# Samples' recurrent states in three pairs of buffers, with each pair's update one step behind its product with C

## Chip, core and metric

The kernel runs on one core of one Trainium2 chip. The metric is device time in microseconds (us) of one execution, taken as the median of several runs. Engines are named as in the profile: PE (TensorE; PEld is its weight load), DVE (VectorE), ACT (ScalarE), POOL (GpSimd) and SP (SyncE, which here only issues DMAs).

## Reference, cut to what matters

One decoder layer is applied to 256 prompt tokens and to 8 samples of 8 new tokens each, 320 token columns in all. The layer is `x + RMSNorm(W_out [chunkMLP | SSD])`, followed by `x + RMSNorm(ConvFFN)`. The change lies in the SSD part (a state-space recurrence) of the eight samples. There are 32 heads in 4 groups of 8; a head has a state of 64 x 128 numbers per sample, and a group has one B and one C vector (128 numbers) per token:

```
h_t = exp(dt_t a) h_{t-1} + dt_t x_t B_t^T        y_t = h_t C_t
```

Written for all 8 tokens of a sample at once, the kernel needs two things of each old state h: the product of h with the sample's C (a part of y), and the new state `h * exp(sum of dt a) + sum over tokens of (decay dt x) B^T`, which is an output (`ssm_state_sample`).

## The kernel before

**Tiling.** All activations lie transposed: 128 features on the partitions, 320 tokens along the row. Every weight is fetched in slabs of 128 x 1024 fp32 (`slab`, L108 to L119). SP issues the load into `wraw`; ACT casts it to a rounded part `whi` (L117); DVE subtracts to get the rest `wlo` (L119); PE makes three matmuls per 128 x 128 block (`accumulate`, L128 to L130). Each of these three tiles has three buffers, and each slab feeds 24 matmuls. These slabs have a raised priority in the scheduler.

**Order of the work.** `project` (PSUM tiles `ps`) multiplies the input by 512 columns of a weight, and `chunk_out` (PSUM tiles `pd`) multiplies 512 mixed features by W_out. Both call `tick()` between slabs. A tick advances the first generator in the list `bg` to its next `yield`, so the small work of the SSD is strewn between the large matmuls. From 440 us of the span on, the program is: `heads_in(1)` (the convolution's projection of the next group, 5 ticks), `chunk_out` 3 (16 ticks), `heads_out(0)` (the projection z, 12 ticks), and so on around for groups 1 to 3. Each group's `ssd(g)` is one generator; `z_evac` drains what is left of it (`finish(tasks[g])`). The scheduler that lays the instructions out (one fixed order per engine) goes by priority and by when operands and buffers come free, so a load whose buffer is free may be issued well ahead of its place in the program.

**The states.** A state tile `st` is 128 x 512 fp32 (256 KB): one sample, one group. Samples i and 4+i form pair i. Five buffers hold `st`. `ssd(g)` does:

- `load_state(i)` (L729): SP loads the two tiles of a pair.
- `fourfold` (L353): ACT copies the sample columns of x (for one group) and of B (once, at the start) four times over, for the 32 tokens of one half of the samples; PE then transposes (`by_token`, L351). One tile `x4` of 4 KB per partition holds both halves.
- `times` (L746): DVE multiplies a transposed x in PSUM by dt; `xq` is the result for the samples and shares the buffer of `x4`. ACT casts all of `xq` to `xsp` (L788), and DVE subtracts on 64 partitions (L789). `xsp` is the moving operand of every state update of the group.
- `decayed` (L780): POOL makes `xde`, one buffer, which PE multiplies for the prompt's state (`s1`, L797).
- For each pair i: `picked` (L811, ACT: B masked to the sample), `with_c` (L803, PE: C times the pair, into `ps_yo`), `shrunk` (L816, POOL: the state times its decay), `grown` (L821, PE makes `up_ps`, DVE adds it to the state), `store_state` (L828, ACT issues the two stores), then the load of pair i+2. Two yields per pair.
- `ps_yo` goes into `xdt` (L861); then eight heads of decay matrices (`decays`, L870, with their rows `cs` loaded by SP in `load_sums`) and `products` (L890, `y_ps`, L898).

**The last group.** For g = 3 the loop does only `with_c`. The generator `renewals` loads all of group 3's states a second time and updates them during `chunk_out` 6 and 7; its last pair is updated in the hand-over between the two halves of the layer, where `next(rest[0])` (L1004) stands and POOL issues the stores.

Of the kernel before, what the change touches and what calls it, by code (L numbers as in the profile page):

```python
# [2 lines left out]

# [6 lines left out]
F32 = mybir.dt.float32  # L10
F32R = mybir.dt.float32r
I32 = mybir.dt.int32
AF = mybir.ActivationFunctionType
ALU = mybir.AluOpType
# [3 lines left out]
P = 128  # L18
NP = 256
NB, TS = 8, 8  # L20
NS = NB * TS
NT = NP + NS
# [12 lines left out]
def hybrid_step(  # L35
# [10 lines left out]
    act, dve, pool, pe, sp = nc.scalar, nc.vector, nc.gpsimd, nc.tensor, nc.sync  # L46
# [10 lines left out]
    def misc(name):  # L57
        return ms.tile([P, 512], F32, tag="ms", name=name)
# [79 lines left out]
    bg = []  # L138
# [210 lines left out]
    def by_token(ps, x, c):  # L349

        pe.transpose(ps, x[:, P * c:P * c + P], ident)  # L351

    def fourfold(out, x):  # L353

        for i in range(2):
            act.copy(out[:, :, i], x[:, :, 32 * i:32 * i + 32].unsqueeze(2).to_broadcast([P, 4, 4, 32]))
        return out.rearrange("p k i q t -> p k (i q t)")

    with ExitStack() as mctx:
        op = mctx.enter_context(tc.tile_pool(name="op", bufs=1))  # L360
# [335 lines left out]
        with tc.tile_pool(name="sd", bufs=1) as sd:  # L696
# [4 lines left out]
            cb, cms = shared[:, :NT + NS], shared[:, NT + NS:].rearrange("p (b i) -> p b i", b=NB)  # L701
            pool.tensor_copy(cb[:NS, :NS], ident[:NS, :NS])
            pool.tensor_copy(cb[NS:, NT:], ident[NS:, NS:])
            x4 = fourfold(sd.tile([P, 4, 2, 4, 32], F32, tag="x4", name="b4", bufs=1), bT[:, :, NP:NT])
            for c in range(4):
                ps = misc("bt_ps")
                for g in range(4):
                    by_token(ps[:, P * g:P * g + P], (bT if c < 2 else x4)[:, g], c % 2)
                if c < 2:
                    act.copy(btok[:, c, :], ps)  # L710
                else:
                    b = bsp[:, c - 2]
                    act.copy(b, ps)
                    for rs in (slice(32, 64), slice(96, P)):
                        dve.tensor_tensor(out=b[rs], in0=ps[rs], in1=b[rs].bitcast(F32), op=ALU.subtract)

            def by_head(ap):
                return ap.rearrange("p (h d) -> p h d", d=64)
# [4 lines left out]
            def ssd(g):  # L723
# [4 lines left out]

                def load_state(i):  # L729

                    st = [sd.tile([P, 512], F32, tag="st", name="st", bufs=5) for _ in range(2)]
                    for h in range(2):
                        sp.dma_start(st[h], state_ssm[4 * h + i, g])
                    return st
# [5 lines left out]
                    sp.dma_start(cs, dacs_d[h0 + 2 * j:h0 + 2 * j + 2, o:o + NT].unsqueeze(0).broadcast_to([P, 2, NT]))  # L740
                    return cs

                sts = [load_state(i) for i in range(2)]

                xdt = sd.tile([P, 3, 512], F32, tag="xdt", name="xdt", bufs=1)
                def times(out, ps, c, at=slice(0, P), h=slice(0, 8)):  # L746
                    n = h.stop - h.start
                    dve.tensor_tensor(out=by_head(out), in0=by_head(ps),
                                      in1=dt[at, c, h0 + h.start:h0 + h.stop].unsqueeze(2).to_broadcast([at.stop - at.start, n, 64]), op=ALU.mult)
                x4 = fourfold(sd.tile([P, 4, 2, 4, 32], F32, tag="x4", name="x4", bufs=1), xs[:, :, NP:NT])  # L750
                turned = []
                for c in range(4):
                    ps = misc("xt_ps")
                    for j in range(4):
                        by_token(ps[:, P * j:P * j + P], (xs if c < 2 else x4)[:, j], c % 2)
                    if c < 2:
                        times(xdt[:, c, :], ps, c)
                    else:
                        turned.append(ps)
                xq = sd.tile([P, 2, 512], F32, tag="x4", name="xq", bufs=1)  # L760
                for i, ps in enumerate(turned):
                    times(xq[:, i, :], ps, 3 + i)
                    for r in range(2):
                        at = slice(64 - 64 * r + 32 * i, 96 - 64 * r + 32 * i)
                        times(xdt[at, 2, 256 * r:256 * r + 256], ps[at, 256 * r:256 * r + 256], 2, at, slice(4 * r, 4 * r + 4))
# [12 lines left out]
                yield  # L778

                def decayed(i, c):  # L780
                    xde = sd.tile([P, 512], F32, tag="xde", name="xde", bufs=1)
                    pool.tensor_tensor(out=by_head(xde), in0=by_head(xdt[:, c, :]),
                                      in1=dec[:, i, h0:h0 + 8].unsqueeze(2).to_broadcast([P, 8, 64]), op=ALU.mult)
                    return xde

                x0d = decayed(0, 0)
                xsp = sd.tile([P, 2, 512], F32R, tag="xsp", name="xsp", bufs=1)
                act.copy(xsp, xq)  # L788
                dve.tensor_tensor(out=xsp[64:], in0=xq[64:], in1=xsp[64:].bitcast(F32), op=ALU.subtract)  # L789
                for hb in range(2):  # L790
                    dve.tensor_tensor(out=cms[:, 4 * hb:4 * hb + 4], in0=cmask[:, 4 * hb:4 * hb + 4],
                                      in1=cT[:, g, NP + 32 * hb:NP + 32 * hb + 32].unsqueeze(1).to_broadcast([P, 4, 32]),
# [18 lines left out]
                def picked(i):  # L811
                    bm = sd.tile([P, 2, P], F32R, tag="bm", name="bm", bufs=2)
                    act.activation(bm, bsp[:, :, bs].bitcast(F32), AF.Copy, scale=bsel[:, i:i + 1])
                    return bm

                def shrunk(i, st):  # L816
                    for h in range(2):
                        pool.tensor_tensor(out=by_head(st[h]), in0=by_head(st[h]),
                                           in1=tote[:, h0:h0 + 8, 4 * h + i:4 * h + i + 1].to_broadcast([P, 8, 64]), op=ALU.mult)

                def grown(st, bm):  # L821
                    for h in range(2):
                        ps = misc("up_ps")
                        made = pe.matmul(ps, bm[:, h], xsp[:, h], start=True, stop=True)
                        dve.tensor_tensor(out=st[h], in0=st[h], in1=ps, op=ALU.add)
                    return made.ins

                def store_state(i, st, by=act):  # L828
                    for h in range(2):
                        by.dma_start(o_ssm_s[4 * h + i, g], st[h])  # L830

                def renewals():
                    sts = [load_state(i) for i in range(2)]
                    yield
                    for i in range(4):
                        st, bm = sts.pop(0), picked(i)
                        shrunk(i, st)
                        yield
                        made = grown(st, bm)
                        store_state(i, st, act if i < 3 else pool)  # L840
                        if i < 2:
                            sts.append(load_state(2 + i))
                        yield made

                for i in range(4):
                    if g < 3:
                        bm = picked(i)
                    yield
                    st = sts.pop(0)
                    with_c(i, st)  # L850
                    yield
                    if g < 3:
                        shrunk(i, st)
                        grown(st, bm)
                        store_state(i, st)
                    if i < 2:
                        sts.append(load_state(2 + i))

                for r in range(2):
                    at = slice(64 * r, 64 * r + 64)  # L860
                    dve.tensor_tensor(out=by_head(xdt[at, 2, 256 * r:256 * r + 256]), in0=by_head(ps_yo[at, :256]),  # L861
                                      in1=ed[at, g, :].unsqueeze(2).to_broadcast([64, 4, 64]), op=ALU.mult)

                made = {}

# [61 lines left out]
                    (pool if g == 3 else act).dma_start(o_ssm_p[g], s1)  # L927
                    yield
                if g == 3:
                    rest.extend([renewals(), final()])  # L930
                    next(rest[0])
                else:
                    yield
                    yield
                    for _ in final():
                        pass
# [49 lines left out]
            norm = heads_out(2, 2, 3)  # L986
            norm3 = heads_out(3, 3, 2)
            finish(norm)
            bg.append(chain(repeat(None, 1), islice(rest[0], 4)))
            chunk_out(w_out, 6, *res[2], False, rate=2)  # L990
            finish(norm3)
            sq2 = hp.tile([P, NT], F32, tag="ssq", name="sq2")

            bg.append(islice(rest[0], 3))
            squares, one = squares_of(sq2)
            chunk_out(w_out, 7, *res[3], False, squares)

# [3 lines left out]

            with first():
                with tc.issue_after(pd_last[-1]):
                    made = next(rest[0])  # L1004
                with tc.issue_after(made):
                    most = token_sums(sq2)
                with tc.issue_after(sums_ins[-1]):
                    ps = token_sums(*one)
                with tc.issue_after(sums_ins[-1]):
                    made = next(rest[1])  # L1010
                r = rsqrt_by_root(most, ps, 1.0 / D)
                behind = rsqrt_ins[-1]
                with tc.issue_after(behind):
                    next(rest[1])
                with tc.issue_after(made):
                    r2b = spread(r)
# [254 lines left out]
```

## Time and profile before

| what | value |
|---|---|
| median of 3 runs | 1811.76 us (1810.66 to 1812.52) |
| profiled execution, device time | 1810.5 us |
| its span, first to last instruction | 1808.8 us |
| PE, PEld busy | 1781.4 us (98%), 1743.8 us (96%) |
| DVE, ACT, POOL busy | 1183.7, 793.7, 294.7 us |
| granted PE clock, mean | 0.995 |
| DMA | 294.66 MB, mean 163 GB/s |
| loads of `st` | 40 of 256 KB, median 3.9 us from issue to landing |
| stores of `st` | 32 of 256 KB |

How to read it: the times of the profile belong to one execution, whose own time is 1.7 us above its span and 1.3 us below the median. A busy time can hide waits of other engines; where a wait matters is seen in the stretch of time where it falls. The SSD work of the four groups lies between 440 and 750 us of the span, the updates of group 3 between 808 and 853 us.

### The profile page before, as it was taken

The numbers are of one execution on the slowest core, as the hardware profiler recorded it, in microseconds if no ns is written. First come the engines' busy times: TensorE is split into PE (matmuls) and PEld (weight loads), VectorE is DVE, ScalarE is ACT, GpSimd is POOL, SyncE is SP. The second block draws the span as 40 slices with busy tenths as digits, with TensorE's granted clock in tenths as the row PEclk, the third lists the DMA queues.
The fourth block names the chain that finished last, engine by engine and source line by source line (L and its number), as shares of the span: only waits on it lengthen the run. The fifth ranks groups of instructions, "written<-read, shape, count | busy, mean of one in ns | idle before, by whom it ended". The sixth has DMA issues, their size and how long they took to land.

```text
span 1808.8 us, 31156 instructions
## 1 busy us (share of the span) xinstructions
PE 1781.4 (98%) x12200; PEld 1743.8 (96%) x12200; DVE 1183.7 (65%) x2044; ACT 793.7 (44%) x1100; POOL 294.7 (16%) x619
## 2 busy tenths in 40 slices
PE   8999999999999999999999999999999999999998
PEld 7999999999889889999999999999999999999997
DVE  4449664556977968677885464747565565756575
ACT  5444454334535445444554433333434343433335
POOL 2102200000431312104421010101101010101004
PEclk9999999999999999999999999999999999999999
DMA  8656544555565565546554545455545445554542
GB/s 270 187 142 188 171 133 153 153 155 176 196 192 187 165 203 172 159 156 212 161 155 154 154 147 153 148 153 153 154 152 153 145 154 150 155 150 152 149 151 103
DMA packets 222947, 294.66 MB, mean 163 GB/s; under 512 B 16752, under 2 KB 150736, under 8 KB 222608
## 3 DMA queue, kind: packets, MB, share of 16 engines
q1 hardware_dynamic: 210544, 270.21, 49.6%
q10 hardware_dynamic: 9872, 14.82, 2.2%
q0 software_dynamic: 2384, 7.64, 1.4%
q8 instruction: 96, 1.57, 0.4%
q14 instruction: 51, 0.42, 0.1%
HBM read 277.80 MB, written 14.82 MB: 162 GB/s over the span
## 4 chain that ended last, share of the span: by engine, by line
PE 89%; DVE 5%; DMA 3%; issue 1%; ACT 1%; POOL 1%; SPq 0%; ACTq 0%; DVEq 0%; POOLq 0%
PE ps L128 19%; PE ps L130 19%; PE ps L129 19%; PE pd L128 9%; PE pd L130 9%; PE pd L129 9%; DVE wlo L119 2%; DMA cT<-in_x_tok 1%; DMA st<-in_state_ssm 1%; PE y_ps L898 1%; DMA cs<-dacs_d 1%; DMA out_ssm_state_sample<-st 0%; DVE cv L383 0%; DVE cs L883 0%; PE sg L660 0%
## 5 line engine op out<-in xcount | busy, mean ns | idle before, releaser
L119 DVE TENSOR_TENSOR wlo<-wraw,whi 128x1024 fp32r<-128x1024 f32 (+1 forms) x474 | 589.5, 1244 | 443.1 <-ACT whi L117 440.4
L117 ACT CAST whi<-wraw 128x1024 fp32r<-128x1024 f32 (+1 forms) x474 | 494.3, 1043 | 724.7 <-PE ps L129 427.9
L128 PE MATMUL ps<-h_hi,whi 128*128 128x320 f32 x2528 | 786.1, 311 | 5.5 <-ACT whi L117 2.4
L130 PE MATMUL ps<-h_hi,wlo 128*128 128x320 f32 x2528 | 782.8, 310 | 2.5 <-DVE wlo L119 2.5
L129 PE MATMUL ps<-h_lo,whi 128*128 128x320 f32 x2528 | 781.9, 309 | 0.0
L128 PEld LDWEIGHTS ps<-h_hi,whi 128*128 128x128 f32 x2528 | 476.3, 189 | 11.2 <-issue 4.3
L130 PEld LDWEIGHTS ps<-h_hi,wlo 128*128 128x128 f32 x2528 | 476.2, 188 | 4.4 <-DVE wlo L119 4.3
L129 PEld LDWEIGHTS ps<-h_lo,whi 128*128 128x128 f32 x2528 | 476.4, 188 | 0.8 <-issue 0.5
L128 PE MATMUL pd<-fhi,whi 128*128 128x320 f32 x704 | 217.0, 308 | 0.0
L129 PE MATMUL pd<-flo,whi 128*128 128x320 f32 x704 | 217.0, 308 | 0.0
L130 PE MATMUL pd<-fhi,wlo 128*128 128x320 f32 x704 | 217.0, 308 | 0.0
L128 PE MATMUL pd<-ohi,whi 128*128 128x320 f32 x448 | 140.2, 313 | 0.0
L129 PE MATMUL pd<-olo,whi 128*128 128x320 f32 x448 | 138.9, 310 | 0.0
L130 PE MATMUL pd<-ohi,wlo 128*128 128x320 f32 x448 | 138.7, 310 | 0.0
L128 PEld LDWEIGHTS pd<-fhi,whi 128*128 128x128 f32 x704 | 132.1, 188 | 0.0
L129 PEld LDWEIGHTS pd<-flo,whi 128*128 128x128 f32 x704 | 132.1, 188 | 0.0
L130 PEld LDWEIGHTS pd<-fhi,wlo 128*128 128x128 f32 x704 | 132.1, 188 | 0.0
L1082 POOL COPY ptf<-pad 128x2 f32<-128x2 f32 x88 | 21.1, 240 | 620.6 <-DVE pad L1070 620.0
L211 DVE TENSOR_TENSOR acc_ffn<-acc_ffn,pd 128x320 f32<-128x320 f32 x160 | 77.4, 484 | 38.3 <-PE pd L130 36.8
L128 PEld LDWEIGHTS pd<-ohi,whi 128*128 128x128 f32 x448 | 84.1, 188 | 2.9 <-issue 1.6
L130 PEld LDWEIGHTS pd<-ohi,wlo 128*128 128x128 f32 x448 | 84.1, 188 | 1.0 <-issue 1.0
L129 PEld LDWEIGHTS pd<-olo,whi 128*128 128x128 f32 x448 | 84.2, 188 | 0.5 <-issue 0.2
(295 smaller groups left out, 1578.7 us busy)
## 6 DMA issues: line engine op xcount, KB each, us to landing
wraw<-in_ffn_w_up SPq DMA_DIRECT2D x176, 512.0 KB, 3.7
wraw<-in_w_in SPq DMA_DIRECT2D x144, 512.0 KB, 3.8
wraw<-in_ffn_w_down SPq DMA_DIRECT2D x88, 512.0 KB, 3.5
wraw<-in_w_out SPq DMA_DIRECT2D x64, 512.0 KB, 3.5
st<-in_state_ssm SPq DMA_DIRECT2D x40, 256.0 KB, 3.9
out_ssm_state_sample<-st ACTq DMA_DIRECT2D x30, 256.0 KB, 4.0
cs<-dacs_d SPq DMA_DIRECT2D x16, 320.0 KB, 4.5
xr<-in_xT SPq DMA_DIRECT2D x4, 640.0 KB, 4.8
```

Source lines behind the costliest of these rows:

```text
L117: act.copy(hi[:, :m], raw[:, :m])
L119: dve.tensor_tensor(out=lo[:, :m], in0=raw[:, :m], in1=hi[:, :m].bitcast(F32), op=ALU.subtract)
L128: pe.matmul(ps, whi, xhi, start=first, stop=False)
L129: pe.matmul(ps, whi, xlo, start=False, stop=False)
L130: return pe.matmul(ps, wlo, xhi, start=False, stop=last).ins
L211: dve.tensor_tensor(out=acc[:, nb, :], in0=acc[:, nb, :], in1=ps[:, :NT], op=ALU.add)
L898: pe.matmul(ps[64 * i:64 * i + 64, cols], w(hl), x(hl, m, cpx), tile_position=(0, 64 * i), **flags)
L1082: pool.tensor_copy(ptf[:, k, :], pad[:, 256:258])
```

## The change

There are six buffers for `st` (three whole pairs) in place of five, and three pairs are loaded at a group's start. A step of the loop now does `begin(i)` (C times pair i, the mask of B, the decay of the state on POOL) and then `end(i-1)` (update and store of the pair before). The fourth pair is loaded in step 3, when nothing else is begun; it is begun after the loop and ended one tick later. Group 3 does the same as the others, except that its last `end` stays in the hand-over; the second load of its states (`renewals`) and the places that advanced it are gone. A group has two more yields (24 in place of 22 for g < 3, 21 in place of 20 for g = 3).

The room comes from `x4`: `fourfold` now copies one half (i = 0 or 1) into a 2 KB tile with the tag `xde`, which has two buffers instead of one and also holds `xq` (one half) and the products of `decayed`. The cast to `xsp` and the subtraction are made per half, right after that half's `times`, ahead of the group's first yield.

```diff
-    def fourfold(out, x):
-        for i in range(2):
-            act.copy(out[:, :, i], x[:, :, 32 * i:32 * i + 32].unsqueeze(2).to_broadcast([P, 4, 4, 32]))
-        return out.rearrange("p k i q t -> p k (i q t)")
+    def fourfold(out, x, i):
+        act.copy(out.rearrange("p k (q t) -> p k q t", q=4), x[:, :, NP + 32 * i:NP + 32 * i + 32].unsqueeze(2).to_broadcast([P, 4, 4, 32]))
+        return out
...
-            x4 = fourfold(sd.tile([P, 4, 2, 4, 32], F32, tag="x4", name="b4", bufs=1), bT[:, :, NP:NT])
             for c in range(4):
                 ps = misc("bt_ps")
+                b4 = bT if c < 2 else fourfold(sd.tile([P, 4, P], F32, tag="xde", name="b4", bufs=2), bT, c - 2)
                 for g in range(4):
-                    by_token(ps[:, P * g:P * g + P], (bT if c < 2 else x4)[:, g], c % 2)
+                    by_token(ps[:, P * g:P * g + P], b4[:, g], c if c < 2 else 0)
...
-                    st = [sd.tile([P, 512], F32, tag="st", name="st", bufs=5) for _ in range(2)]
+                    st = [sd.tile([P, 512], F32, tag="st", name="st", bufs=6) for _ in range(2)]
...
-                sts = [load_state(i) for i in range(2)]
+                sts = [load_state(i) for i in range(3)]
...
-                x4 = fourfold(sd.tile([P, 4, 2, 4, 32], F32, tag="x4", name="x4", bufs=1), xs[:, :, NP:NT])
-                turned = []
+                xsp = sd.tile([P, 2, 512], F32R, tag="xsp", name="xsp", bufs=1)
                 for c in range(4):
                     ps = misc("xt_ps")
+                    x4 = xs if c < 2 else fourfold(sd.tile([P, 4, P], F32, tag="xde", name="x4", bufs=2), xs, c - 2)
                     for j in range(4):
-                        by_token(ps[:, P * j:P * j + P], (xs if c < 2 else x4)[:, j], c % 2)
+                        by_token(ps[:, P * j:P * j + P], x4[:, j], c if c < 2 else 0)
                     if c < 2:
                         times(xdt[:, c, :], ps, c)
-                    else:
-                        turned.append(ps)
-                xq = sd.tile([P, 2, 512], F32, tag="x4", name="xq", bufs=1)
-                for i, ps in enumerate(turned):
-                    times(xq[:, i, :], ps, 3 + i)
+                        continue
+                    i = c - 2
+                    xq = sd.tile([P, 512], F32, tag="xde", name="xq", bufs=2)
+                    times(xq, ps, c + 1)
+                    act.copy(xsp[:, i], xq)
+                    dve.tensor_tensor(out=xsp[64:, i], in0=xq[64:], in1=xsp[64:, i].bitcast(F32), op=ALU.subtract)
...
-                    xde = sd.tile([P, 512], F32, tag="xde", name="xde", bufs=1)
+                    xde = sd.tile([P, 512], F32, tag="xde", name="xde", bufs=2)
...
-                xsp = sd.tile([P, 2, 512], F32R, tag="xsp", name="xsp", bufs=1)
-                act.copy(xsp, xq)
-                dve.tensor_tensor(out=xsp[64:], in0=xq[64:], in1=xsp[64:].bitcast(F32), op=ALU.subtract)
...
-                def renewals():
-                    sts = [load_state(i) for i in range(2)]
-                    yield
-                    for i in range(4):
-                        st, bm = sts.pop(0), picked(i)
-                        shrunk(i, st)
-                        yield
-                        made = grown(st, bm)
-                        store_state(i, st, act if i < 3 else pool)
-                        if i < 2:
-                            sts.append(load_state(2 + i))
-                        yield made
-
-                for i in range(4):
-                    if g < 3:
-                        bm = picked(i)
-                    yield
-                    st = sts.pop(0)
-                    with_c(i, st)
-                    yield
-                    if g < 3:
-                        shrunk(i, st)
-                        grown(st, bm)
-                        store_state(i, st)
-                    if i < 2:
-                        sts.append(load_state(2 + i))
-
-                for r in range(2):
...
+                def yo_to_xdt():
+                    for r in range(2):
...
+                bms = {}
+
+                def begin(i):
+                    with_c(i, sts[i])
+                    bms[i] = picked(i)
+                    shrunk(i, sts[i])
+
+                def end(i, by=act):
+                    made = grown(sts[i], bms.pop(i))
+                    store_state(i, sts[i], by)
+                    return made
+
+                for i in range(4):
+                    if i < 3:
+                        begin(i)
+                    else:
+                        sts.append(load_state(3))
+                    if i:
+                        end(i - 1)
+                    yield
+                    yield
+                begin(3)
+                yo_to_xdt()
+                yield
+                if g < 3:
+                    end(3)
+                    yield
...
-                    rest.extend([renewals(), final()])
-                    next(rest[0])
+                    rest.extend([lambda: end(3, pool), final()])
...
-            bg.append(chain(repeat(None, 1), islice(rest[0], 4)))
             chunk_out(w_out, 6, *res[2], False, rate=2)
...
-            bg.append(islice(rest[0], 3))
...
-                    made = next(rest[0])
+                    made = rest[0]()
```

More of the change, by code (lines that the diff above doesn't have):

```diff
@@ L1 @@
 from contextlib import ExitStack, nullcontext
-from itertools import chain, islice, repeat
+from itertools import repeat
 import concourse.bass as bass
@@ L845, in ssd @@
-                for i in range(4):
-                    if g < 3:
-                        bm = picked(i)
-                    yield
-                    st = sts.pop(0)
-                    with_c(i, st)
-                    yield
-                    if g < 3:
-                        shrunk(i, st)
-                        grown(st, bm)
-                        store_state(i, st)
-                    if i < 2:
-                        sts.append(load_state(2 + i))
-                for r in range(2):
-                    at = slice(64 * r, 64 * r + 64)
-                    dve.tensor_tensor(out=by_head(xdt[at, 2, 256 * r:256 * r + 256]), in0=by_head(ps_yo[at, :256]),
-                                      in1=ed[at, g, :].unsqueeze(2).to_broadcast([64, 4, 64]), op=ALU.mult)
+                def yo_to_xdt():
+                    for r in range(2):
+                        at = slice(64 * r, 64 * r + 64)
+                        dve.tensor_tensor(out=by_head(xdt[at, 2, 256 * r:256 * r + 256]), in0=by_head(ps_yo[at, :256]),
+                                          in1=ed[at, g, :].unsqueeze(2).to_broadcast([64, 4, 64]), op=ALU.mult)
```

## Prediction

> **What bounds the kernel now.** I read the page first. Section 1 gives the busy time of each engine:
>
> ```profile
> span 1808.8 us, 31156 instructions
> PE 1781.4 (98%) x12200; PEld 1743.8 (96%) x12200; DVE 1183.7 (65%) x2044; ACT 793.7 (44%) x1100; POOL 294.7 (16%) x619
> ```
>
> PE is the bound, and PE's own work stays: the change has the same transposes, products with C and updates. So a gain can only come out of the 27 us in which PE is idle. The second view, busy time by stretch, shows where these lie (columns: length, busy us of each engine with its instructions, granted clock, DMA share, GB/s):
>
> ```profile
> 440.00:700.00 260.00, 251.51 (x1789) 230.12 (x1788) 211.34 (x413) 130.49 (x200) 69.85 (x89) 1.00 0.61 189
> 700.00:850.00 150.00, 149.88 (x1062) 144.01 (x1061) 109.01 (x190) 66.93 (x99) 29.25 (x25) 1.00 0.57 178
> 850.00:858.00 8.00, 5.25 (x32) 4.01 (x31) 7.04 (x20) 2.83 (x6) 1.67 (x3) 0.95 0.48 169
> ```
>
> Groups 0 to 2 (440 to 700 us) have 8.5 us of idle PE at a full clock; group 3's stretch has 0.1 us; the hand-over has 2.75 us. The rest lies at the kernel's two ends, which the change leaves alone. Third, who PE waited for between 440 and 700 us (total, times, longest):
>
> ```profile
> PE yo_ps L808 <- DMA st<-in_state_ssm: 3.8, 4, 1.5
> PE tsum L257 <- DVE ssq L276: 1.2, 1, 1.2
> PE y_ps L898 <- DVE cs L887: 1.2, 2, 0.8
> PE up_ps L824 <- DVE st L825: 1.1, 1, 1.1
> PE up_ps L824 <- DVE xsp L789: 1.1, 1, 1.1
> ```
>
> These five add up to 8.4 us. The largest is C times a pair whose load has not landed. The chain of waits from 615 to 645 us says why (start, length, what):
>
> ```profile
> 626.43 0.61 DVE st L825
> 627.06 5.16 DMA out_ssm_state_sample<-st
> ...
> 633.19 5.69 DMA st<-in_state_ssm
> ...
> 638.92 0.63 PE yo_ps L808 x6
> ```
>
> A buffer must be updated, stored and landed (5.16 us) before the next load of 5.69 us can start in it, and PE stands at the end of that chain. SP waits for such stores too, with weight loads queued behind:
>
> ```profile
> SPq L733 <- DMA out_ssm_state_sample<-st: 33.2, 17, 5.0
> ```
>
> **The change, part by part.**
>
> *Three pairs.* Before, in groups 0 to 2 the second half of pair 2 and all of pair 3 go into buffers of pairs 0 and 1. From C times pair 0 to C times pair 2 there are two steps; the steps lie 4.2 to 4.75 us apart in the trace (528.17, 532.92, 537.68 us), so about 9.2 us. In that time fit the decay on POOL (2 x 1.07), two adds on DVE (2 x 0.68), store (median 3.8) and load (median 3.9): 11.2 us, or 14.4 with the 5.2 and 5.7 us of the chain. The lack of 2 to 5 us is what PE shows. After, only pair 3 reuses a buffer, that of pair 0. Pair 0 is ended in step 1, with its decay long done, and pair 3 is begun in the place of step 4: three steps, 13.5 us, for adds, store and load, 9.1 to 12.3 us. It fits by 1 to 4 us, so I take the 3.8 us as gone, with 0 to 1.5 us (the longest single wait) left for the range.
>
> *Update one step behind.* `up_ps` waited 1.1 us on DVE's add, since PSUM came free late. DVE itself waited 5.0 us for POOL's decay and 4.5 us for `up_ps`. With the update a step behind, the decay is 4 us old when the add comes, so that 1.1 us goes. The first update of group 2 waited 1.1 us for the subtraction that makes `xsp`; the first update now comes one step (4.2 us or more) later, so this goes too. Sum gone: 3.8 + 1.1 + 1.1 = 6.0 us.
>
> The waits `y_ps` on `cs` (1.2) and `tsum` on `ssq` (1.2) are DVE queues with other causes. I leave both as they are; the first may lose up to 1.2 us, since DVE loses its 9.5 us of waiting and SP's load of `cs` at 493.80 us was queued among four loads of `st` that waited for stores.
>
> *Halves.* The ACT copies are the same ten (0.62 us each). The cast to `xsp` becomes eight of 128x512: nearest row, the cast of `bsp`, 0.60, so 8 x 0.60 - 4 x 1.05 = +0.6 us of ACT. The subtraction becomes eight of 64x512: nearest row 0.68 (other two-input operations of that row length), 8 x 0.68 - 4 x 1.22 = +0.6 us of DVE. ACT is half idle in the stretch, DVE is busy 211 of 260 us; both are small. What is new is the chain: x4 half, transposes, `times`, cast, subtract, with buffers handed round among two, and `decayed` taking its buffer from the same two. Queued behind a DVE subtract that waits for its cast are the `wlo` of the next slabs, and PE waits for those. Bounds: nothing, if the cast is done when DVE gets there (the four subtractions before were never waiting); at most 0.60 for the cast plus 1.05 for a slab's cast ahead of it on ACT, 1.65 us per half, 13 us in eight. The nearest row is ACT's one wait of 5.1 us for `xq` in four groups, which passed without a wait of PE right behind it. PE has cover of up to two slabs, 24 matmuls x 0.146 us (their spacing in the trace) = 3.5 us each; it is absent only where DVE is full. I take 1.0 us in all. The one stretch of 12 us where a chain like this cost PE something was 620 to 632 us.
>
> *Group 3.* Eight loads of 256 KB vanish (2.1 MB; no wait of PE hung on them). Eight POOL decays, six adds (6 x 0.68 = 4.1 us of DVE), six `up_ps` (6 x 0.3 = 1.8 us of PE, only moved), four masks (4 x 0.51) and six store issues move from 808 to 834 us to some place between 700 and 770 us. DVE has 109 of 150 us busy there and PE waits for nothing, so: nothing. If the cover were gone it would be the 4.1 us of adds. The two more yields per group push group 3 back by 6 ticks (three slabs, 10 us), so its last heads fall into the projection z of group 3, which has 12 ticks to spare; a Silu evacuation then stands between the exponentials, up to two more table loads of 1.28 us on ACT, which has 67 of 150 us busy: nothing. The hand-over keeps its update, PE waits there for `h_hi` (2.1 us) as before.
>
> *POOL against DVE.* The subtraction L789 took 1.22 us in three groups and 2.05 us in the fourth, at 620.72, when POOL was working on `st` (618.62 for 3.06 us); the wait of 1.1 us above came of that. [...] My sum stays at the one-in-four that is seen.
>
> Sum: -6.0 + 1.0 = -5.0 us. Made against the profiled execution, 1810.5 - 5.0 = 1805.5; the median of the runs is 1.3 us above it, 1811.76 - 5.0 = 1806.8.
>
> **Rivals.**
>
> 1. *All idle of the stretch goes*, `y_ps` and `tsum` too, because DVE no longer waits at all: -8.5 us, 1803.3. For it: DVE's 9.5 us of waiting. Against: the `tsum` wait follows a group's last z column, which is not touched. Chance 0.10.
>
> 2. *Given back on DVE.* The stretches 476 to 488 and 500 to 512 us show DVE at 12.00 of 12 us; the work there stays, so the stalls may only move a slab on, and the halves meet POOL: 8 x 0.83 = 6.6 us at most on DVE, half of it (3.3) on PE. -6.0 + 3.3 = -2.7, about 1809. By the full 6.6 it is +0.6, 1812.4. For it: the full stretches; against: the subtraction moves ahead of the first decay of the group, away from POOL. Chance 0.25.
>
> 3. *The halves stall the weights: slower.* The place is a group's start: DVE, in order, sits at the subtract behind ACT's casts, eight times 1.65 us, and `wlo` comes late in a stretch with DVE full (452 to 464 us: 11.64 of 12). -6.0 + 13.2 = +7.2, 1819. It decides from 1.2 us per half on, (6.0 + 3.6) / 8. Against it: the two slabs of cover, and the transposes of before that were slipped between slab matmuls with gaps of 0.3 us at most. Chance 0.20.
>
> 4. *Not done as said*: pair 3 is loaded late because SP holds it behind weight loads that wait for buffers (100.6 us of such waits in the stretch). Each group then keeps a wait of up to 1.5 us; -6.0 + 1.0 + 4 x 1.0 = -1, 1810.8. Chance 0.05, within 0.2%.
>
> **How the numbers follow.** 0.2% is 3.6 us, about what a measurement of this kernel can tell from no change; the borders are 1808.1 and 1815.4. My forecast, -5.0 with +-1.4 us, has 0.40 and of that a small part above 1808.1; with the first rival and a share of the second at its low end, faster is 0.53. Within 0.2%: the rest of the second rival, the fourth, and the weak form of the third, 0.27. Slower: 0.20. The range begins at the first rival's 1803.2 and goes to 1815.4, where the third becomes decisive; it leaves out the third's upper part and what lies below the stretch's whole idle.
>
> **What would show it.** In the profile after: 32 loads of `st`; no wait of `yo_ps` on `st` over 1 us; none of `up_ps`; DVE without a wait on POOL's decay; idle PE of 440 to 700 us down from 8.5 to about 3.5 us; SP's waits for stores well under 33 us; no more table loads than two over before; the hand-over at 2.7 us of idle PE as now. I am wrong if `xsp` or `x4` shows up as a releaser of PE or of `wlo` by more than 1 us in all, or if idle moves to stretches beyond 700 us.

## The result, and the profile after

The kernel after takes 1802.36 us (median of 6 runs, 1800.27 to 1804.62); the kernel before, run again on the same chip, 1810.43 us (1806.94 to 1812.52). The ratio is 0.9958, 95% interval 0.9948 to 0.9968: 7.6 us faster by the ratio. I had forecast 1806.8 us, a gain of 5.0 us, with a range from 1803.2 to 1815.4. The direction was right. The gain came out larger than forecast, and the time lies 0.8 us below the range. Part of the distance in time is not the change's: the kernel before came out 1.3 us lower here than the 1811.76 us from which I had forecast. The gain itself, 7.6 us, has an interval from 5.8 to 9.4 us, so the 5.0 us of the forecast lie just outside it. The profiled execution took 1801.72 us.

Section 1 of the page after:

```profile
span 1800.0 us, 31160 instructions
PE 1776.3 (99%) x12200; PEld 1742.5 (97%) x12200; DVE 1190.5 (66%) x2048; ACT 797.1 (44%) x1104; POOL 294.3 (16%) x619
```

The number of PE instructions is the same, 12200. Yet the time in which PE counts as busy fell from 1781.4 to 1776.3 us. That is 5.1 of the 8.8 us by which the span is shorter. The busy time by stretch (length, busy us of PE, PEld, DVE, ACT and POOL with their instructions, clock, DMA share, GB/s):

```profile
440.00:700.00 260.00, 254.72 (x1835) 237.50 (x1834) 220.42 (x415) 133.60 (x205) 65.60 (x87) 1.00 0.62 195
700.00:838.00 138.00, 137.84 (x986) 131.47 (x985) 103.57 (x187) 63.09 (x94) 30.43 (x26) 1.00 0.53 162
```

Idle PE from 440 to 700 us went from 8.5 to 5.3 us, 3.2 us less where I had expected 5. Whom PE waited for there (total, times, longest):

```profile
PE up_ps L822 <- DVE st L823: 2.8, 1, 2.8
PE s_ps L795 <- POOL xde L783: 1.5, 3, 0.7
PE y_ps L899 <- DVE cs L888: 0.7, 2, 0.4
PE tsum L257 <- DVE ssq L276: 0.2, 1, 0.2
```

The waits of `yo_ps` on a state's load are gone. A wait of `up_ps` on DVE's add is still there, and longer than before. A new one is `s_ps` on `xde`. The waits of `tsum` and `y_ps`, which I had left as they were, fell from 2.4 to 0.9 us. In sum: -3.8 (`yo_ps`), -1.1 (`up_ps` on `xsp`), +1.7 (`up_ps` on the add), +1.5 (`s_ps`), -1.5 (`tsum` and `y_ps`), which is -3.2 us. So the recorded waits alone say that the change did less than I thought, while the measured time says that it did more.

### The profile page after: what moved, and what is told of

Its sections match the earlier page's. It is cut to its first block, busy times and chain, and to the rows that moved or that the text cites. A ratio compares the mean times of both kernels' runs of the same rounds, so it can differ in the third digit from the quotient of the medians.

```text
span 1800.0 us, 31160 instructions
## 1 busy us (share of the span) xinstructions
PE 1776.3 (99%) x12200; PEld 1742.5 (97%) x12200; DVE 1190.5 (66%) x2048; ACT 797.1 (44%) x1104; POOL 294.3 (16%) x619
## 4 chain that ended last, share of the span: by engine, by line
PE 92%; DVE 4%; DMA 2%; ACT 1%; issue 1%; POOL 0%; ACTq 0%; SPq 0%; DVEq 0%; POOLq 0%
PE ps L128 20%; PE ps L130 19%; PE ps L129 19%; PE pd L128 10%; PE pd L130 10%; PE pd L129 10%; DMA wraw<-in_w_in 1%; DVE wlo L119 1%; PE y_ps L899 1%; PE yo_ps L806 0%; PE up_ps L822 0%; PE sg L659 0%; ACT whi L117 0%; DMA out_ssm_state_sample<-st 0%; PE tsum L257 0%
```

## Where the time came from: PE's visits to the small work

To see it I took PE's matmuls in order of time, from 443.0 us to the `spread` in the hand-over, which is the same place in every version. Slab matmuls follow each other at 0.146 us. Whenever PE leaves them for other matmuls, I count a visit: the time from the last slab matmul's slot to the second slab matmul after, less two slots. The recorded idle time in a visit is taken off. This is my own working from the trace (the ends of visits leave some choice, worth a few tenths of a us):

| | before | after | difference |
|---|---|---|---|
| hand-over's `spread` at | 855.22 us | 846.93 us | -8.3 |
| visits | 67 | 53 | -14 |
| recorded idle in visits | 8.3 us | 5.2 us | -3.1 |
| visits, without that idle | 67.5 us | 63.2 us | -4.4 |
| of these, visits with `yo_ps`, `up_ps` or `s_ps` | 27.3 us | 24.0 us | -3.3 |
| slabs and the rest | 336.4 us | 335.6 us | -0.8 |

Half of the gain is thus work of the same instructions that takes less time, in fewer visits. The lines of PE in order of time show how (start, length, engine and line, operation, tiles, shape, count, in brackets the idle time before and its releaser). Before, around group 2:

```profile
623.55 0.64 PE L808 MATMUL yo_ps<-st,cb_cms 128*32 128x256 f32 x8
628.30 0.62 PE L808 MATMUL yo_ps<-st,cb_cms 128*32 128x256 f32 x2
631.95 0.63 PE L808 MATMUL yo_ps<-st,cb_cms 128*32 128x256 f32 x6 [1.52 <-DMA st<-in_state_ssm]
635.37 0.62 PE L808 MATMUL yo_ps<-st,cb_cms 128*32 128x256 f32 x2
638.92 0.63 PE L808 MATMUL yo_ps<-st,cb_cms 128*32 128x256 f32 x6 [0.97 <-DMA st<-in_state_ssm]
```

The eight matmuls of a pair that is whole take 0.64 us (first line). They are the records of four calls of `with_c`, two for each call, and they run side by side: in the first line, four start within 0.02 us (623.550 to 623.570 us), one for each of the four `tile_position`s, and the other four 0.24 us later (623.790 to 623.810 us). In a split pair the fixed order of PE's instructions has the first call, which needs only the first tile (2 records), mostly some slab matmuls, then the other three calls (6 records). Each part takes 0.62 or 0.63 us by itself, since even one call has a record in each of the two rounds. The second and the third line cost 1.25 us in place of 0.64, and only the 1.52 us right before the third line is called idle. Before, four pairs were split so, and a fifth, at 544.08 us, was stretched to 1.28 us. After, the same group:

```profile
621.54 0.64 PE L806 MATMUL yo_ps<-st,cb_cms 128*32 128x256 f32 x8
625.83 0.64 PE L806 MATMUL yo_ps<-st,cb_cms 128*32 128x256 f32 x8
630.59 0.64 PE L806 MATMUL yo_ps<-st,cb_cms 128*32 128x256 f32 x8
639.32 0.64 PE L806 MATMUL yo_ps<-st,cb_cms 128*32 128x256 f32 x8
```

All 16 pairs come whole. A whole product with the update behind it is a visit of 1.23 us. By that measure the visits with split, stretched or interrupted groups of before held 4.2 us too much, beside the 6.0 us of recorded waits. How close it is shows at the fourth pair, the only one that within its group reuses a buffer in the kernel after: its second tile lands 0.8 us before PE takes it up in group 3 (729.03 and 729.80 us) and 1.0 us in group 2, against 13 and 37 us in groups 0 and 1.

## The experiments

The ratios are to the kernel before, whose median was 1808.9 to 1809.4 us in those series. A difference "in us" is the ratio's share of 1810 us, good to about 1.6 us either way against the kernel before, and to 2.2 to 2.7 us between two of the other kernels. Theory A is that of the section above: what paid is that no product with C meets a pair that is not there.

### The halves alone

```diff
 (fourfold, x4, xq, xsp, xde as in the change; everything else as before)
-                    xde = sd.tile([P, 512], F32, tag="xde", name="xde", bufs=1)
+                    xde = sd.tile([P, 512], F32, tag="xde", name="xde", bufs=2)
```

> The kernel before with the halved copies alone (x4 and xq by halves in the two xde buffers, cast and subtraction per half); five state buffers, the old steps and the second load of group 3 stay. Theory A (the gain lies in the states' buffers: waits for a pair that has not landed, and the splitting of its eight matmuls into 2 and 6 that goes with them): no gain, 0 to +3 us against before; yo_ps still waits some 4 us on st. Theory B (part of the unforeseen gain is in the halves, since PE makes the transposes and the B-C products in fewer visits): -1 to -2 us. The prediction's own term for this part was +1.0 us.

Measured: 0.9999 (0.9991 to 1.0008), -0.2 us. Its trace has the new wait of `s_ps` on `xde` (1.6 us), fewer visits for the transposes and the B-C products (12, where the kernel before has 15), and still five split pairs. The time fits theory A, but its sign doesn't: `yo_ps` waits 2.0 us for `st` and not some 4, two of the split pairs wait for nothing, and `up_ps` no longer waits for `xsp`. The 1 to 2 us of theory B aren't seen in the times, which cannot rule out 1 us either; in the trace the hand-over comes 1.2 us earlier than before, although 11 matmuls at half the clock (last section) cost 1.3 us on the way.

### Six buffers, old steps

```diff
-                    st = [sd.tile([P, 512], F32, tag="st", name="st", bufs=5) for _ in range(2)]
+                    st = [sd.tile([P, 512], F32, tag="st", name="st", bufs=6) for _ in range(2)]
...
-                sts = [load_state(i) for i in range(2)]
+                sts = [load_state(i) for i in range(3)]
...
-                    if i < 2:
-                        sts.append(load_state(2 + i))
+                    if i == 0:
+                        sts.append(load_state(3))
```

> halves_only with six state buffers, three pairs loaded at a group's start and the fourth after the first step; each pair still updated in the step of its own product, group 3 still loaded a second time. Theory A: the waits of yo_ps on st go, and with them the split groups, idle PE and busy PE fall by about 4 us each: -6 to -8 us against halves_only; the waits of up_ps stay. Theory C (the gain comes of the update being one step behind): no more than the 3.8 us of recorded idle goes here, the rest only in the kernel after. Theory D (the second load): under -2 us here.

Measured: 0.9979 (0.9970 to 0.9987), 1805.53 us, -3.6 us against halves_only: half of what theory A expected, and within theory C's bound of 3.8, though not for its reason. One pair of group 2 still waits, 1.8 us, and is the only one of the five that is still split; so the recorded waits of `yo_ps` fell by 0.2 us alone. The hand-over comes 4.7 us earlier in the trace than in halves_only; 1.7 us of that is recorded idle and the other 3 us is busy time, nearly all in visits with `yo_ps`, `up_ps` or `s_ps` (27.5 us in halves_only, 24.6 us here). So the larger part of what the buffers brought is invisible in the list of waits.

### Without the second load of group 3

```diff
...
-                    if g < 3:
-                        shrunk(i, st)
-                        grown(st, bm)
-                        store_state(i, st)
+                    shrunk(i, st)
+                    if g < 3 or i < 3:
+                        grown(st, bm)
+                        store_state(i, st)
...
-                    rest.extend([renewals(), final()])
-                    next(rest[0])
+                    rest.extend([last, final()])
```

> six_buffers without the second load of group 3: its pairs are updated in the step of their product, as in the other groups, only the last add and store stay in the hand-over. Theory A: within 1 us of six_buffers, since PE waited for nothing from 700 to 850 us. Theory D (the gain beyond the forecast is the second load and the updates beside it that are gone): -3 us or more against six_buffers.

Measured: 0.9996 (0.9988 to 1.0005), 1808.07 us, 3.1 us slower than six_buffers. Neither theory had this. Group 3's stretch, in which PE had waited for nothing, now has waits (700 to 840 us):

```profile
PE up_ps L821 <- DVE xsp L762: 1.0, 1, 1.0
PE yo_ps L805 <- DMA st<-in_state_ssm: 0.6, 1, 0.6
```

The second load was not waste: with the update in the product's own step, putting off group 3's updates was worth 3 us. These two waits are 1.6 us of it; for the rest the trace names no single place.

### One step behind, with the second load

```diff
                 def begin(i):
                     with_c(i, sts[i])
-                    bms[i] = picked(i)
-                    shrunk(i, sts[i])
+                    if g < 3:
+                        bms[i] = picked(i)
+                        shrunk(i, sts[i])
...
-                    if i:
+                    if i and g < 3:
                         end(i - 1)
...
-                    rest.extend([lambda: end(3, pool), final()])
+                    rest.extend([renewals(), final()])
+                    next(rest[0])
```

> The kernel after for groups 0 to 2, with group 3 as before: products only, then a second load and the updates during chunk_out 6 and 7. Beside no_reload and six_buffers it makes a square: the update in its own step or one behind, with or without the second load. Theory C (the gain of one step behind lies in groups 0 to 2): within 1.5 us of after, some 4 us under six_buffers. Theory F (one step behind pays in group 3 alone, where the update in its own step made PE wait): about six_buffers, 3 to 4 us above after.

Measured: 0.9968 (0.9957 to 0.9979), 1802.91 us, 2.0 us under six_buffers and 1.8 us above the kernel after; the intervals overlap with those of both. The square is now complete (us against before):

| | second load kept | second load gone |
|---|---|---|
| update in its own step | -3.8 | -0.7 |
| update one step behind | -5.8 | -7.6 |

The time lies halfway between the forecasts of theories C and F, so it doesn't decide between them. One step behind is worth 2.0 us with the second load, within the error of the two ratios, and 6.9 us without, which is clear of it. The two parts of the change depend on each other: dropping the second load costs 3.1 us alone, and gains 1.8 us (again within the error) once updates trail. The trace leans to theory C: the hand-over comes 0.9 us later than in the kernel after, and nine matmuls at half the clock (last section), which the profiled execution of that kernel does not have between 440 us and the hand-over, account for 1.1 us.

### One step behind, with five buffers

```diff
-                    st = [sd.tile([P, 512], F32, tag="st", name="st", bufs=6) for _ in range(2)]
+                    st = [sd.tile([P, 512], F32, tag="st", name="st", bufs=5) for _ in range(2)]
```

> The kernel after with five state buffers instead of six and all else as it is: the second tile of pair 2 has to wait for the store of pair 0, which now comes a step later. Theory A: the waits of yo_ps on st come back, larger than before, and the groups split again: +5 to +10 us against the kernel after, of which only about half is recorded as idle PE. Theory C (update one step behind): most of the gain stays, not more than +3 us against after.

Measured: 1.0026 (1.0015 to 1.0036), 1813.89 us: 12.3 us above the kernel after, beyond theory A's upper end. Three pairs wait and are split, and a fourth is split without a wait:

```profile
PE yo_ps L806 <- DMA st<-in_state_ssm: 6.4, 3, 2.3
```

Against after, the hand-over comes 13.6 us later: 6.3 us of recorded idle, 3.6 us of busy time in visits, and 3.6 us in the slabs themselves, of which the last section speaks. About half is recorded idle, as theory A said; one buffer decides the sign of the whole change.

### Product and update in different ticks

```diff
-                    if i:
-                        end(i - 1)
                     yield
+                    if i:
+                        end(i - 1)
                     yield
```

> The kernel after, with the product of pair i in the first tick of a step and the update of pair i-1 in its second, so that PE makes them in more separate visits. Theory E (what counts is the number of visits, each with a fixed price of some 0.3 us): +2 us or more against after. Theory A (a visit costs what its matmuls cost, 0.77 us for eight yo_ps, 0.46 us for two up_ps, 1.23 us together; only waits and split groups cost more): within 1 us of after, plus 0.5 us for each group of eight that comes out split.

Measured: 1.0029 (1.0018 to 1.0040), 1814.56 us, 12.9 us above after; both theories expected far less. The visits are not the cause, for there are hardly more (56 against 53); so theory E's price for a visit was not put to the test either. The trace shows a different cause: the update of pair 0 comes later by more than the half step of the edit, and with it the store and the fourth pair's load. In group 3, counted from the first product, the second store leaves at 13.8 us in place of 8.7; in group 0, where DVE is full, pair 0's first add comes at 483.59 us in place of 465.78. In group 3 (start, length and so on as above):

```profile
733.88 0.62 PE L806 MATMUL yo_ps<-st,cb_cms 128*32 128x256 f32 x2 [1.15 <-DMA st<-in_state_ssm]
738.11 1.08 PE L806 MATMUL yo_ps<-st,cb_cms 128*32 128x256 f32 x6 [3.61 <-DMA st<-in_state_ssm]
```

The 1.08 us of the second line, where such six took 0.63 us in the kernel before, are matmuls at half the clock: the slab matmuls behind them are 0.27 us apart in place of 0.146 us. In all 7.1 us are waits of `yo_ps` on `st`. The slack that the prediction put at 1 to 4 us is 0.8 us in this group of the kernel after, and the later store uses it up.

### Three attempts at the waits that are left

In the kernel after, DVE has no gap when `up_ps` waits 2.8 us for it (475 to 488 us), since the add stands behind convolution work of raised priority. The wait on `xde` comes from `xq` holding both buffers. First, `decayed` writes into `s1`:

```diff
...
-                x0d = decayed(0, 0)
+                s1 = sd.tile([P, 512], F32, tag="s1", name="s1", bufs=1)
+                x0d = decayed(0, 0, s1)
...
```

> The kernel after, with the first product of decayed written into the tile s1 (free until the product of it is copied there) instead of a buffer of xde, so that it need not wait for xq. Theory A: the waits of s_ps on xde go (1.5 us of recorded idle, some 2.5 us with what is hidden): -1 to -2.5 us against after. Against it: nothing, if the wait only moves to the next DVE result.

Measured: 0.9985 (0.9977 to 0.9994), 1806.51 us, 4.9 us slower than after. The three waits on `xde` became one of 1.9 us on `s1`, and a wait of `tsum` on DVE of 3.1 us appeared. Why DVE is late there was not found out. Two of its waits, 2.8 and 3.1 us, are followed by 25 matmuls at half the clock, 3.0 us lost, which the profiled execution of the kernel after does not have between 440 us and the hand-over.

Second, the same with the adds raised:

```diff
-                        dve.tensor_tensor(out=st[h], in0=st[h], in1=ps, op=ALU.add)
+                        with first():
+                            dve.tensor_tensor(out=st[h], in0=st[h], in1=ps, op=ALU.add)
```

> x0d_in_s1 and, in addition, the state's two adds on DVE at the raised priority that the PSUM evacuations have, so that up_ps gets its PSUM back in group 0. The wait of up_ps on DVE (2.8 us, the longest left in the kernel after) should go: -3 to -5 us against after in all, about 1798 us if the other queues on DVE have room; 0 or more if the evacuations that now come later hold up PE in turn.

Measured: 0.9945 (0.9933 to 0.9957), 1799.24 us, 2.4 us under after, where 3 to 5 were expected. Third, the raised adds alone on the kernel after:

> The kernel after with the state's adds at the raised DVE priority alone (the first product of decayed stays in xde). If the 2.8 us wait of up_ps in group 0, and the half-rate matmuls that can follow it, are worth what the traces suggest: -3 to -4 us against after; the waits of s_ps on xde (1.5 us recorded) stay, so 0 to 2 us above both_fixes.

Measured: 0.9945 (0.9931 to 0.9959), 1799.01 us, 10 us under the kernel before. It is 2.4 us under the kernel after (3 to 4 were expected), but the intervals of the two overlap by 0.0011, so that this difference isn't shown by the times. From 440 to 700 us PE waits only here:

```profile
PE s_ps L795 <- POOL xde L783: 1.5, 3, 0.7
PE y_ps L900 <- DVE cs L889: 0.2, 1, 0.2
```

The 2.8 us wait of `up_ps` is gone. So the place for `x0d` brought nothing on top of the adds; raising the adds is clear of the error against x0d_in_s1 (7.2 us), and not against after. This is the fastest version that I found. Is the adds' place in DVE's queue then the real cause of what the change gained? The kernel after itself speaks against it: there `up_ps` waits longer for the add than before. Two more kernels test it. On the kernel before:

> The kernel before with the state's adds at the raised DVE priority. If the buffers are the limit (theory A): the wait of up_ps goes (1.1 us), stores leave a little earlier, the waits of yo_ps on st stay in part: -1 to -3 us against before. If the adds' late place in DVE's queue was the whole cause: -6 us or more, as much as the change itself.

Measured: 0.9982 (0.9973 to 0.9991), 1805.78 us, -3.3 us, slightly more than theory A's -1 to -3 and less than half of what the change gains. `yo_ps` still waits four times for `st`, 1.9 us together. On no_reload:

> no_reload (six buffers, update in the step of its own product) with the adds at the raised priority. If one step behind pays because a pair's add is then no longer late in DVE's queue, this gets most of it: -4 to -6 us against no_reload, close to after. If it pays because PE no longer follows POOL's decay and DVE's add within one step: -1 to -2 us only, the waits of yo_ps and up_ps stay.

Measured: 0.9998 (0.9989 to 1.0006), 1808.26 us, no change against no_reload: neither forecast holds. With six buffers and the update in its own step, raised adds give nothing in the time. The trace is less plain: `yo_ps` no longer waits for `st`, nor `up_ps` for the add, and recorded idle up to the hand-over falls by 1.2 us, but two waits of 1.8 and 1.6 us are followed by 26 matmuls at half the clock, 3.0 us lost, of which no_reload's trace has none in that stretch; a few more follow the wait of 2.0 us (last section). Two of the waits in the place of the old ones:

```profile
PE up_ps L821 <- DVE xsp L762: 2.0, 1, 2.0
PE y_ps L882 <- DVE xdt L845: 1.8, 1, 1.8
```

This fits the reading that one step behind pays because it takes PE's update out of the step in which it would follow `xsp`, POOL's decay and DVE's add at once. No run separates the three.

## Why the prediction was off

The terms of the sum, along one path through the experiments (halves, buffers, one step behind in groups 0 to 2, second load gone):

| step of the prediction | forecast | measured | ratios compared |
|---|---|---|---|
| halves | +1.0 | -0.2 | 0.9999 to 1 |
| three pairs | -3.8 | -3.6 | 0.9979 to 0.9999 |
| update one step behind | -2.2 | -2.0 | 0.9968 to 0.9979 |
| group 3 | 0 | -1.8 | 0.9958 to 0.9968 |
| sum | -5.0 | -7.6 | |

The two large terms came out as forecast, in total, though only "three pairs" is clear of its error. The miss of 2.6 us lies in "halves" and "group 3", neither beyond its own error, so by the times it isn't settled how it divides between the two. The traces, one execution each, put it into "halves": along the path the hand-over's `spread` comes at 855.22, 854.03, 849.30, 847.78 and 846.93 us, and from 443 us up to there halves_only and behind_reload lost 1.3 and 1.1 us at half the clock, the others nothing. Without these the steps are -2.5, -3.5, -2.6 and +0.2 us. What can be said:

- **"PE's own work stays ... so a gain can only come out of the 27 us in which PE is idle."** This step failed. The instructions stayed, their time didn't: 5.1 us of the gain lie in busy time. The range's lower end was built on it ("all idle of the stretch goes", 1803.2), and so it was too high. Rival 1 came nearest in its number, but for a wrong reason: 5.3 us of the 8.5 are still idle.
- **Three pairs.** The mechanism was right in the kernel after: the loads land in time, 32 in all, and no pair is split. The size of -3.8 was the recorded idle of four waits of `yo_ps`; in the step that brings the buffers, these waits fell by 0.2 us alone (2.0 to 1.8), and the 3.6 us measured are 1.7 us of idle, mostly of other waits, and more of pairs that are no longer split. That the size fits is luck. The slack of "1 to 4 us" is 0.8 and 1.0 us in groups 3 and 2.
- **Update one step behind.** `up_ps` was to lose its wait on the add ("the decay is 4 us old when the add comes, so that 1.1 us goes"). It didn't: it grew to 2.8 us. POOL was never the cause in group 0; DVE's queue was, as before_adds_first and adds_first show, in which this wait is gone. The wait on `xsp` did go, but it is gone in halves_only already, where the subtraction comes earlier and the update doesn't trail. So of the two waits of this term, one stayed and the other went by another part of the change; that -2.0 us were measured is luck, and within the error.
- **Halves.** The chain through ACT never held up `wlo` or PE: no such wait in the trace. The cost lies where I named it in half a sentence ("`decayed` taking its buffer from the same two"): 1.5 us of `s_ps` waiting. It is paid back in halves_only by the waits of `yo_ps` on `st` (3.8 to 2.0 us) and of `up_ps` on `xsp` (1.1 us, gone), and a little by fewer visits: the transposes and the B-C products take 14.9 us in 12 visits, after 15.4 us in 15. The prediction had none of this in its +1.0.
- **Group 3, "nothing".** Wrong by itself: dropping the second load alone costs 3.1 us (no_reload). It costs nothing only together with the trailing update.
- **Rivals 2 to 4.** DVE full at 476 to 488 us did keep one stall (rival 2's place), at a smaller price than the gain. Its 0.83 us for a subtraction that meets POOL is 2.05 less 1.22 us, one of four in the trace before. After, four of the eight took 0.67 to 0.69 us, and the four at whose start POOL was at work on `xde` 1.22 to 1.42 us, 2.8 us more in all on DVE, where I had put 6.6 us at most; PE waited nowhere for `xsp`. Nothing of rival 3 was seen, nor of rival 4: `yo_ps` waits nowhere. SP's waits for stores did not fall, 35.2 us after 33.2, and cost PE nothing; I had taken them for a part of the loss.
- As said: no wait of DVE on POOL's decay, 15 table loads from 440 to 860 us as before, the hand-over's `h_hi` wait 2.1 us.

## What to carry to other kernels

On a bound engine, "idle" isn't all that a wait costs: here the eight short matmuls of a pair ran side by side in 0.64 us, and once cut for a late operand each part took 0.62 or 0.63 us, which the profile books as busy. Sum visit times of like groups (0.64 us whole against 1.25 us split) before setting a lower bound on the time. When a buffer's chain of update, store and load is the limit, write down its slack in steps; here one buffer, or an update put off by half a step in the program, moved the result by 12 us. A small edit also moves the whole order of the instructions: one that should have gained 1 to 2.5 us cost 4.9 us (x0d_in_s1), so an effect of that size needs a trace that shows its place.

## What the runs showed of the hardware

A long wait of PE can be followed by a slow stretch. In x0d_in_s1 the same wait of `up_ps` as in the kernel after, here 2.85 us, is followed by slab matmuls at 0.27 us instead of 0.146 us:

```profile
485.19 0.63 PE L823 MATMUL up_ps<-xsp,bm 128*128 128x512 f32 x1 [2.85 <-DVE st L824]
485.61 0.47 PE L129 MATMUL pd<-olo,whi 128*128 128x320 f32 x1
485.88 0.47 PE L130 MATMUL pd<-ohi,wlo 128*128 128x320 f32 x1
```

The windows around it show a granted clock (third number from the end) of one half:

```profile
486.00:487.00 1.00, 1.00 (x6) 1.00 (x5) 1.00 (x2) 0.36 (x1) 0.00 (x0) 0.50 0.69 260
490.00:500.00 10.00, 10.00 (x81) 9.14 (x80) 9.22 (x17) 4.93 (x7) 3.06 (x2) 1.00 0.76 260
```

Nine to thirteen matmuls run so in most of these stretches, some 1.3 us lost after the wait is over. In behind_five there are three (the clock is 0.50 from 544 to 546 us in one), beside three waits of `yo_ps` of 2.3 us at most. In halves_only the matmuls follow a wait of 1.45 us (`tsum`). In no_reload_adds_first they follow waits of 1.8 us (`y_ps`), 1.6 us (`tsum`, with its six narrow matmuls in between) and 2.0 us (`up_ps`; the eight `yo_ps` behind it took 1.08 us, whole pairs elsewhere 0.64 us). In the hand-over the wait of 2.1 us for `h_hi` is followed by a longer stretch in the kernels before and after alike: the slab matmuls are 0.27 us apart up to 863.6 and 855.3 us.

The length of the wait does not settle it in these traces. Behind the 2.8 us of `up_ps` in the profiled execution of the kernel after the clock is 1.00 from 485 to 488 us, and the slab matmuls keep their 0.146 us. In the kernel before the clock is 0.50 from 247 to 249 us, and PE's only wait in the 3 us of small matmuls ahead of that is 0.4 us. What sets it off was not shown.

The times of the runs carry it too. Of the six executions of the kernel after, the two with a mean granted clock of 0.997 took 1800.3 us each, the two with 0.995 took 1803.3 and 1804.6 us. The mean over a kernel's executions is 0.9960 for after, 0.9944 for behind_reload, 0.9939 for behind_five, 0.9928 for split_ticks and 0.9948 for x0d_in_s1. A mean lower by 0.001 is at most 1.8 us (an estimate: 0.001 of 1800 us, if PE is the bound all the time). By it, some 4 of the 12.3 us of behind_five, some 6 of the 12.9 us of split_ticks, 2 of the 4.9 us of x0d_in_s1 and all of the 1.8 us of behind_reload can be lost clock: a wait costs its length, and sometimes half the clock after it.
